# Half-size TensorE tiles in pairs for the half-filled and block-diagonal products of a hybrid decoder's mixing stage

## The chip, the cores and the metric

The kernel runs on one core of a Trainium2 chip. The metric is the time of one launch on the device in microseconds, the median over runs; lower is better.

## The reference

One trunk layer of a decoder with three groups of heads, for 256 prompt tokens and 8 sequences of 8 sample tokens, 320 token columns in all, in fp32:

```
hn = rms_norm(x);  proj = hn @ w_in                     # 2048 -> 6656
y_rw  = rwkv7_mix(...)   # 12 heads x 64: S = S*w_t + (S a_t) b_t' + v_t k_t',  y = S r_t
y_hg  = hgrn2_mix(...)   # 6 heads, 128 x 128 state: S = f_t S + k_t v_t',  o = q_t S
y_lru = rglru_mix(...)   # 512 channels, gated linear recurrence behind a convolution
x = x + concat(y_rw, y_hg, y_lru) @ w_out
hn = rms_norm(x); gate, val = split(hn @ w_up)          # 2 x 5632
x = x + (silu(causal_conv(gate)) * val) @ w_down;  y = rms_norm(x)
```

It returns the outputs of all tokens and the new states of all groups (for HGRN2 `p_hgrn` of the prompt and `s_hgrn` of the samples).

## The kernel before, in words

Channels lie on the 128 partitions, tokens in the free dimension. Every projection (`gemm`) streams its weights in chunks of 8 blocks of 128 x 128 (512 KB) on the SP queue, splits each chunk into a high and a low part on ScalarE (L173) and VectorE (L174), and makes three products of 320 columns for each block: high by high (L198), high by low (L199), and, after the eight blocks of the chunk, low by high (L205). These run on the whole array.

The recurrences are written as products over chunks of 64 tokens. RWKV heads go in pairs, one on each half of the partitions (`half[0]`, `half[1]`); six pairs alternate with six HGRN heads, then two pairs of RG-LRU tiles. Their products are plain fp32. The chains of steps (`rwkv_operands`, `rwkv_chunks`, `rwkv_norm`, `hgrn_steps`, `lru_steps`) are Python generators: `gemm` advances a virtual clock by a fixed cost for each projection product and calls `tick`, which emits the next step of a chain when its due time (the number that it yielded, such as `L_EV = 1.5` or `L_EX = 4.0`) has passed. So steps of the chains are emitted between projection products in a fixed order. The compiler's scheduler then orders each engine's instructions by this order and by when it takes their operands to be ready, and may let an instruction that isn't ready be overtaken by later ones. On the chip each engine goes through its own list in order.

The products that the change and the prediction speak of:

- L445, L447: decay and in-context rate of a pair, `lw` by `lora`. Only 64 of the 128 rows of each stationary operand are not zero (the first half for one, the second for the other).
- L541: products of all pairs of tokens in a chunk, on row halves, into two aux tiles; L551 the same for the samples on the whole array. VectorE masks them into `mt1` and `mt2`. `mt1` goes to DRAM (L569) and back as diagonal 16 x 16 blocks (L570), VectorE inverts these by substitution (L574, L576), and the result goes to DRAM (`du`, L577) and back as `U` (L578). L644 transposes `U` to `T`.
- L584, L594, L603, L610: token-major operands, by products with the identity; L584 on column halves (128x64), L594 on tiles of 64x32, all four into one aux tile, L603 transposes on row halves into two aux tiles.
- L636, L638: the right-hand sides `rq`. For each head and each half of the chunks a transpose on a row half, then a product of `mt2` (zero outside two 64 x 64 blocks) with `vsw`, on the whole array.
- L659, L664, L668: the doubling of the inverse from blocks of 16 to 32 and from 32 to 64. Each is four products with a 128 x 128 operand whose two diagonal 64 x 64 blocks alone are not zero. In the first round L659, L664 and L668 run, in the second L659 and L664.
- L683, L686: `pq` from `U`. L707, L709: outputs without a state, one product on the whole array, one on a column half, alternating. L716: 64x64 tiles, six products.
- L863, L867: HGRN's products of token blocks. L934, L935: transposes of `v` and `kd` to token-major `vt` and `kt`; the 64 sample tokens fill half the rows of the third block, POOL clears the other half (L931). L948 to L953: outputs. L980, L981: `p_hgrn`. L986: the sample states, for four of the eight sequences at a time, `kt` (half filled) by `hex` of 512 columns, which VectorE builds by a mask (L974); L987 adds the result to `hs`, and POOL's queue stores it (L988). L832 loads the next head's `hs` on the same queue.

An aux tile is one PSUM bank of 512 fp32 on 128 partitions. There are four of the kind `aux_r` (RWKV) and two `aux_h` (HGRN, RG-LRU); two more banks are the projections' `acc`.

Of the kernel before, what the change touches and what calls it, by code (L numbers as in the profile page):

```python
# [17 lines left out]
P = 128  # L18
D = 2048
NK = D // P  # L20
TP = 256
# [32 lines left out]
for _name, _w in (  # L54
    ("ident", 128), ("ones", 128), ("bones", 128), ("bswap", 128), 
    ("psw", 128), ("eye2", 64), ("bm", 8), ("bm4", 4),
):
    CST[_name] = (_n, _w)
    _n += _w
# [7 lines left out]
def kernel(ctx: ExitStack, tc: tile.TileContext, i: dict, o: dict):  # L67
# [15 lines left out]
    # ------------------------------------------------------------- constants  # L83
# [12 lines left out]
    # -------------------------------------------------------- weight streaming  # L96
# [29 lines left out]
    def advance(kind):  # L126
        """One more step of the first chain of a kind; False if it waits for something else."""
# [57 lines left out]
    def behind(out, in_):  # L185
        """A load that doesn't go ahead of the weights that are asked for by now."""
        tc.keep_in_program_order(SY.dma_start(out=out, in_=in_))
# [49 lines left out]
    # ------------------------------------------------------------------ input  # L237
# [95 lines left out]
    # ------------------------------------------------------------ RWKV-7 group  # L333
# [54 lines left out]
    # five 128 x 128 matrices in DRAM, with steps that make their diagonal 16 x 16 blocks one pattern  # L388
# [11 lines left out]
    # sample tokens by half of the batches, then by head, block-diagonal in the heads  # L400
# [11 lines left out]
    # the halves of the columns that stay zero  # L412
# [27 lines left out]
    def rwkv_operands(p, lw, box):  # L440
        while state["pairs"] < p - 1:
            yield None
        # decay and in-context rate
        ps_w = aux_r()
        PE.matmul(ps_w[:, :T], lw[:, 0, :], lora, start=True, stop=True)  # L445
        ps_a = aux_r()
        PE.matmul(ps_a[:, :T], lw[:, 1, :], lora, start=True, stop=True)  # L447
# [78 lines left out]
    def rwkv_chunks(p, lw, box):  # L526
# [7 lines left out]
        # products of all pairs of tokens in a chunk  # L534
# [24 lines left out]
        # inverse of the unit triangles: blocks of 16 by substitution, then doubled  # L559
# [20 lines left out]
        # token-major operands  # L580
# [33 lines left out]
        # the sample tokens  # L614
# [16 lines left out]
        rq = rp.tile([P, 4, P], F32, tag="h", name="rq", bufs=BH)  # L631
        for e in range(2):
            ps = aux_r()
            for m in range(2):
                c0 = m * P + e * 64
                PE.transpose(ps[:, c0:c0 + 64], flat(AR[half[e], 0, 2 * m:2 * m + 2, :]), ident[half[e], half[e]])  # L636
                c0 = m * P + (1 - e) * 64
                PE.matmul(ps[:, c0:c0 + 64], mt2[:, 0, 2 * e + m, :], vsw[:, m, (1 - e) * 64:(1 - e) * 64 + 64],  # L638
                          start=True, stop=True)
            S.copy(flat(rq[:, 2 * e:2 * e + 2, :]), ps[:, 0:256])  # L640
# [5 lines left out]
        for h, Z in zip((16, 32), Zs):  # L646
            def part(t, j):
                """Of each 2h columns the first (j = 0) or the second half."""
                return t.rearrange("p b (n j s) -> p b n j s", j=2, s=h)[:, :, :, j, :]
# [5 lines left out]

            yield L_EV
            ps = aux_r()
            for b in range(4):
                PE.matmul(ps[:, b * 64:(b + 1) * 64], mt1[:, 0, b, :], part(Ts[:, b:b + 1, :], 0), start=True, stop=True)  # L659
# [3 lines left out]
            for b in range(4):  # L663
                PE.matmul(ps_u[:, b * 64:(b + 1) * 64], Z[:, b, :], part(Us[:, b:b + 1, :], 1), start=True, stop=True)  # L664
            if h == 16:
                ps_t = aux_r()
                for b in range(4):
                    PE.matmul(ps_t[:, b * 64:(b + 1) * 64], Us[:, b, :], part(Z[:, b:b + 1, :], 0), start=True, stop=True)  # L668
# [32 lines left out]
        # outputs that need no state, and what the state is multiplied with  # L701
        ps_y = aux_r()
        for e in range(2):
            for m in range(2):
                b = 2 * e + m
                c0 = e * 256 + m * P
                PE.matmul(ps_y[:, c0:c0 + P], pq[:, b, :], mt1[:, 1, b, :], start=(b == 0), stop=False,  # L707
                          skip_group_check=True)
                PE.matmul(ps_y[half[1 - e], c0:c0 + P], vsw[:, m, (1 - e) * 64:(1 - e) * 64 + 64],  # L709
                          mt2[:, 1, b, :], start=False, stop=(m == 0), skip_group_check=True)  # L710
# [17 lines left out]
        # states of both heads, block-diagonal with the heads' columns swapped  # L728
# [46 lines left out]
    def rwkv_norm(p, lw, y, bo):  # L775
        yield L_EV
        # group norm, bonus, gate
# [24 lines left out]
    # ------------------------------------------------------------- HGRN2 group  # L802
# [24 lines left out]
    def hgrn_steps(n, box):  # L827
# [28 lines left out]
        def pairs(lhs, rhs, h, w):  # L856
            """Products of the columns' first with their second halves, h wide (all with all if h = 2)."""
# [13 lines left out]
        # blocks of four, from their middles  # L871
# [40 lines left out]
        # b is now summed over each whole sequence  # L912
# [16 lines left out]
        for src, dst in ((v, vt), (kd, kt)):  # L929
            yield L_HG  # L930
            G.memset(dst[64:P, 2, :], 0.0)  # L931
# [3 lines left out]
            PE.transpose(ps[0:64, 2 * P:3 * P], src[:, TP:T], ident)  # L935
            S.copy(dst[:, 0:2, :].rearrange("p a b -> p (a b)"), ps[:, 0:TP])
            S.copy(dst[0:64, 2, :], ps[0:64, 2 * P:3 * P])
# [31 lines left out]
        # states  # L969
        S.activation(dsam, b[:, TP + ST - 1:T:ST], AF.Exp)  # L970
        for q4 in range(2):
            c = slice(4 * q4, 4 * q4 + 4)
            ex = rp.tile([P, 4, P], F32, tag="hb", name="hex", bufs=BHB)
            V.tensor_tensor(ex, bcast(vt[:, 2, :], 4), cc("bm")[:, c].unsqueeze(2).to_broadcast([P, 4, P]), op=ALU.mult)  # L974
            sn = s0[q4]
            V.tensor_tensor(sn, sn, dsam[:, c].unsqueeze(2).to_broadcast([P, 4, P]), op=ALU.mult)
            yield L_EX
            if q4 == 0:
                ps = aux_h()
                PE.matmul(ps[:, 0:P], kt[:, 0, :], vt[:, 0, :], start=True, stop=False)  # L980
                PE.matmul(ps[:, 0:P], kt[:, 1, :], vt[:, 1, :], start=False, stop=True)  # L981
                pst = rp.tile([P, P], F32, tag="hcr", name="pst", bufs=1)
                S.copy(pst, ps[:, 0:P])
                G.dma_start(out=o["p_hgrn"][n], in_=pst)
            ps = aux_h()
            PE.matmul(ps, kt[:, 2, :], ex.rearrange("p b v -> p (b v)"), start=True, stop=True)  # L986
            V.tensor_tensor(sn, ps.rearrange("p (b v) -> p b v", v=P), sn, op=ALU.add)  # L987
            G.dma_start(out=o["s_hgrn"][n, :, c, :], in_=sn)  # L988

    # ------------------------------------------------------------ RG-LRU group  # L990
# [103 lines left out]
    # -------------------------------------------------------- operands of w_out  # L1094
# [37 lines left out]
    # ------------------------------------------------- output projection + norm  # L1132
# [34 lines left out]
    # --------------------------------------------------------------------- FFN  # L1167
# [94 lines left out]
def _constants():  # L1262
# [31 lines left out]
    put("bm", ((r % 64 // 8)[:, None] == np.arange(8)[None, :]).astype(f))  # L1294
# [101 lines left out]
```

## Time and profile before

| | before |
|---|---|
| median of 3 runs | 1670.26 us (1669.49 to 1672.36) |
| profiled execution, its span | 1670.6 us (the page gives no time around it) |
| PE busy | 1636.4 us, 98% |
| weight loads busy | 1588.0 us, 95% |
| VectorE, ScalarE, POOL busy | 989.1 us, 836.3 us, 151.4 us |
| DMA | 238.83 MB, 143 GB/s in the mean |

PE is TensorE's row of matmuls, PEld that of its weight loads, DVE VectorE, ACT ScalarE, POOL GpSimd, SP the queue that streams the weights. An fp32 product leaves two records in the trace, a transpose one. Durations of single records overlap, since products are pipelined; what a group costs is read from the end of one to the end of the next, as the chain of waits does. A shape such as 64*128 is the tile of the array, rows by columns. The mixing stage lies between about 45 and 636 us.

### The profile page before, as it was taken

What the parts mean: (1) busy time and instruction counts of PE and PEld (TensorE: products, weight loads), DVE (VectorE), ACT (ScalarE), POOL (GpSimd) and SP (SyncE); (2) the same over time, 40 slices, a digit from 0 to 9 for tenths busy, and PEclk for the clock granted to TensorE, in tenths of its full rate; (3) what the DMA queues carried; (4) which work ended last, traced back from release to release, by engine and by line L of the source; (5) the groups of instructions that cost most, each with busy time, mean ns of one, the idle gap of its engine ahead of it and who ended that gap; (6) DMA issues with size and microseconds to landing.
All of it is one profiled execution on the core that took longest, in us unless ns stands there. A gap on an engine that the chain in (4) does not pass through costs nothing.

```text
span 1670.6 us, 28501 instructions
## 1 busy us (share of the span) xinstructions
PE 1636.4 (98%) x11220; PEld 1588.0 (95%) x11220; DVE 989.1 (59%) x1958; ACT 836.3 (50%) x1310; POOL 151.4 (9%) x369
## 2 busy tenths in 40 slices
PE   7899999999999999999999999999999999999996
PEld 7898999999899899999999999999999999999996
DVE  7677677777677656555555555333455555554444
ACT  7675767676766774444433343333333444434442
POOL 3001010101010210000000000000000000000000
PEclk9999999999999999999999999999999999999998
DMA  8434343434344445554454554555545555554553
GB/s 269 138 110 122 110 130 109 131 103 120 108 121 117 145 154 161 151 160 148 147 149 151 151 152 146 151 149 152 150 151 151 151 151 150 148 156 147 150 153 106
DMA packets 87101, 238.83 MB, mean 143 GB/s; under 512 B 16568, under 2 KB 30312, under 8 KB 86968
## 3 DMA queue, kind: packets, MB, share of 16 engines
q1 hardware_dynamic: 82072, 221.67, 44.6%
q0 software_dynamic: 4896, 15.36, 2.7%
q8 instruction: 88, 1.44, 0.4%
q14 instruction: 45, 0.37, 0.1%
HBM read 225.62 MB, written 11.37 MB: 142 GB/s over the span
## 4 chain that ended last, share of the span: by engine, by line
PE 93%; DVE 2%; DMA 2%; ACT 2%; issue 1%; SPq 0%; DVEq 0%; ACTq 0%
PE acc L205 27%; PE acc L198 27%; PE acc L199 27%; DMA U<-du 1%; PE aux_h L867 1%; PE aux_h L953 1%; PE aux_r L659 1%; PE aux_h L986 1%; PE aux_r L664 1%; DVE wl L174 1%; PE aux_r L707 1%; PE aux_r L638 1%; PE aux_r L709 1%; DMA xr<-in_xT 0%; DMA raw<-in_w_in 0%
## 5 line engine op out<-in xcount | busy, mean ns | idle before, releaser
L173 ACT CAST wh<-raw 128x1024 fp32r<-128x1024 f32 (+2 forms) x412 | 421.7, 1024 | 526.2 <-PE acc L199 319.5
L198 PE MATMUL acc<-xh,wh 128*128 128x320 f32 x2208 | 671.1, 317 | 1.0 <-DVE ext L342 1.0
L199 PE MATMUL acc<-xl,wh 128*128 128x320 f32 x2208 | 656.3, 310 | 0.0
L174 DVE TENSOR_TENSOR wl<-raw,wh 128x1024 fp32r<-128x1024 f32 (+2 forms) x412 | 489.9, 1190 | 238.2 <-PE acc L205 114.5
L198 PEld LDWEIGHTS acc<-xh,wh 128*128 128x128 f32 x2208 | 416.3, 189 | 6.5 <-issue 2.6
L199 PEld LDWEIGHTS acc<-xl,wh 128*128 128x128 f32 x2208 | 416.4, 189 | 4.2 <-issue 2.4
L205 PE MATMUL acc<-xh,wl 128*128 128x320 f32 x2208 | 385.3, 315 | 0.0
L205 PEld LDWEIGHTS acc<-xh,wl 128*128 128x128 f32 x2208 | 338.1, 189 | 4.1 <-issue 1.1
L198 PE MATMUL acc<-hh,wh 128*128 128x320 f32 x704 | 207.9, 308 | 0.0
L199 PE MATMUL acc<-hl,wh 128*128 128x320 f32 x704 | 207.8, 308 | 0.0
L199 PEld LDWEIGHTS acc<-hl,wh 128*128 128x128 f32 x704 | 132.1, 188 | 0.0
L198 PEld LDWEIGHTS acc<-hh,wh 128*128 128x128 f32 x704 | 131.7, 187 | 0.0
L205 PE MATMUL acc<-hh,wl 128*128 128x320 f32 x704 | 118.8, 308 | 0.0
L1183 POOL COPY ncch<-fe 128x18 f32<-128x18 f32 x44 | 49.1, 1115 | 652.2 <-DVE fe L1182 652.2
L205 PEld LDWEIGHTS acc<-hh,wl 128*128 128x128 f32 x704 | 107.1, 187 | 0.0
L1193 DVE TENSOR_TENSOR fv<-acc,rstd 128x320 f32<-128x320 f32 x44 | 21.6, 492 | 98.3 <-PE acc L205 98.3
L1181 DVE TENSOR_TENSOR fe<-acc,rstd 128x256 f32<-128x256 f32 x44 | 18.7, 425 | 100.3 <-PE acc L205 100.3
L214 ACT CAST hh<-fv 128x320 fp32r<-128x320 f32 x44 | 20.3, 461 | 96.9 <-DVE fv L1195 96.9
L198 PE MATMUL acc<-yhl,wh 128*128 128x320 f32 x224 | 66.1, 309 | 0.5 <-ACT yhl L214 0.5
L199 PE MATMUL acc<-yhl,wh 128*128 128x320 f32 x224 | 66.2, 309 | 0.0
L1188 DVE SCALAR_TENSOR_TENSOR fc<-fe,prm,fc 128x336 f32<-128x336 f32 x88 | 49.7, 565 | 1.6
L1186 ACT ACTIVATE fc<-fe,prm 128x336 f32<-128x336 f32 x44 | 29.5, 669 | 35.5 <-DVE fe L1182 34.7
(414 smaller groups left out, 1723.1 us busy)
## 6 DMA issues: line engine op xcount, KB each, us to landing
raw<-in_w_up SPq DMA_DIRECT2D x176, 512.0 KB
raw<-in_w_in SPq DMA_DIRECT2D x100, 512.0 KB
raw<-in_w_dn SPq DMA_DIRECT2D x64, 512.0 KB
raw<-in_w_out SPq DMA_DIRECT2D x32, 512.0 KB
raw<-in_w_dn SPq DMA_DIRECT2D x32, 384.0 KB
out_s_hgrn<-hs POOLq DMA_DIRECT2D x12, 256.0 KB, 2.6
hs<-in_hs POOLq DMA_DIRECT2D x10, 256.0 KB, 4.5
x<-in_xT POOLq DMA_DIRECT2D x16, 160.0 KB, 3.0
```

The costliest lines, as they stand in the source:

```text
L173: S.copy(wh[:, ks, :], raws[n][:, ks, :])
L174: V.tensor_tensor(wl[:, ks, :], raws[n][:, ks, :], wh[:, ks, :].bitcast(F32), op=ALU.subtract)
L198: PE.matmul(ps[:, :T], wh[:, k, :], xh[k0 + k], start=st, stop=False)
L199: PE.matmul(ps[:, :T], wh[:, k, :], xl[k0 + k], start=False, stop=False)
L205: PE.matmul(ps[:, :T], wl[:, k, :], xh[k0 + k], start=False, stop=en)
L214: S.copy(xh, src)
L638: PE.matmul(ps[:, c0:c0 + 64], mt2[:, 0, 2 * e + m, :], vsw[:, m, (1 - e) * 64:(1 - e) * 64 + 64], start=True, stop=True)
L1181: V.tensor_tensor(e[:, 2:258], ps[:, 0:TP], rstd[:, 0:TP], op=ALU.mult)
L1183: G.tensor_copy(ncch[:, j], e[:, 248:EX].rearrange("p (b s) -> p b s", s=10)[:, :, 8:10])
L1186: S.activation(c[:, 0:N], e[:, 0:N], AF.Identity, scale=pc("fw", 3 * j), bias=pc("fb", j))
L1188: V.scalar_tensor_tensor(c[:, 0:N], e[:, m:m + N], pc("fw", 3 * j + m), c[:, 0:N], op0=ALU.mult, op1=ALU.add)
L1193: V.tensor_tensor(val, ps[:, :T], rstd, op=ALU.mult)
```

## The change

- `rwkv_operands`: the two products take only the filled row half each, one after the other, into two aux tiles.
- rq: first the four transposes, then the products with `mt2`, each as two of 64x64, one for each block that is not zero; then both copies.
- The doubling: a helper `blocks` makes each of the four products as two of 64x64, on the two diagonal tiles, into the two halves of the partitions of one aux tile.
- Outputs without a state: the four whole products first, then the four on column halves.
- HGRN: POOL copies the 64 sample tokens of `v` and `kd` twice side by side (`both`), and the third transpose takes all 128 columns, so that both halves of the rows are filled with the same tokens; ScalarE copies the result in one instruction. `hex` is built once, with a mask that gives the first four sequences to the first half of the rows and the other four to the second. `p_hgrn` is made a step earlier than the sample states, whose two products take one row half each, one after the other, into two aux tiles.

The mask constant `bm` of 8 columns gives way to `bmx` of 4; comments are taken out as well, which is left out here.

```diff
@@ rwkv_operands
-        ps_w = aux_r()
-        PE.matmul(ps_w[:, :T], lw[:, 0, :], lora, start=True, stop=True)
-        ps_a = aux_r()
-        PE.matmul(ps_a[:, :T], lw[:, 1, :], lora, start=True, stop=True)
+        ps_w, ps_a = aux_r(), aux_r()
+        for n, ps in enumerate((ps_w, ps_a)):
+            PE.matmul(ps[:, :T], lw[half[n], n, :], lora[half[n], :], start=True, stop=True)
@@ rwkv_chunks
+        pss = [aux_r(), aux_r()]
+        for m in range(2):
+            for e in range(2):
+                c0 = m * P + e * 64
+                PE.transpose(pss[e][:, c0:c0 + 64], flat(AR[half[e], 0, 2 * m:2 * m + 2, :]), ident[half[e], half[e]])
         for e in range(2):
-            ps = aux_r()
             for m in range(2):
-                c0 = m * P + e * 64
-                PE.transpose(ps[:, c0:c0 + 64], flat(AR[half[e], 0, 2 * m:2 * m + 2, :]), ident[half[e], half[e]])
                 c0 = m * P + (1 - e) * 64
-                PE.matmul(ps[:, c0:c0 + 64], mt2[:, 0, 2 * e + m, :], vsw[:, m, (1 - e) * 64:(1 - e) * 64 + 64],
-                          start=True, stop=True)
-            S.copy(flat(rq[:, 2 * e:2 * e + 2, :]), ps[:, 0:256])
+                for q in range(2):
+                    k, c = half[1 - q], half[q]
+                    PE.matmul(pss[e][c, c0:c0 + 64], mt2[k, 0, 2 * e + m, c], vsw[k, m, (1 - e) * 64:(1 - e) * 64 + 64],
+                              start=True, stop=True)
+        for e in range(2):
+            S.copy(flat(rq[:, 2 * e:2 * e + 2, :]), pss[e][:, 0:256])
...
+            def blocks(ps, lhs, rhs, j):
+
+                for b in range(4):
+                    r = part(rhs[:, b:b + 1, :], j)
+                    for q in half:
+                        PE.matmul(ps[q, b * 64:(b + 1) * 64], lhs[q, b, q], r[q], start=True, stop=True)
+
             yield L_EV
             ps = aux_r()
-            for b in range(4):
-                PE.matmul(ps[:, b * 64:(b + 1) * 64], mt1[:, 0, b, :], part(Ts[:, b:b + 1, :], 0), start=True, stop=True)
+            blocks(ps, mt1[:, 0], Ts, 0)
...
-            for b in range(4):
-                PE.matmul(ps_u[:, b * 64:(b + 1) * 64], Z[:, b, :], part(Us[:, b:b + 1, :], 1), start=True, stop=True)
+            blocks(ps_u, Z, Us, 1)
             if h == 16:
                 ps_t = aux_r()
-                for b in range(4):
-                    PE.matmul(ps_t[:, b * 64:(b + 1) * 64], Us[:, b, :], part(Z[:, b:b + 1, :], 0), start=True, stop=True)
+                blocks(ps_t, Us, Z, 0)
...
-        for e in range(2):
-            for m in range(2):
+        for b in range(4):
+            PE.matmul(ps_y[:, b * P:b * P + P], pq[:, b, :], mt1[:, 1, b, :], start=(b == 0), stop=False,
+                      skip_group_check=True)
+        for m in range(2):
+            for e in range(2):
                 b = 2 * e + m
-                c0 = e * 256 + m * P
-                PE.matmul(ps_y[:, c0:c0 + P], pq[:, b, :], mt1[:, 1, b, :], start=(b == 0), stop=False,
-                          skip_group_check=True)
-                PE.matmul(ps_y[half[1 - e], c0:c0 + P], vsw[:, m, (1 - e) * 64:(1 - e) * 64 + 64],
+                PE.matmul(ps_y[half[1 - e], b * P:b * P + P], vsw[:, m, (1 - e) * 64:(1 - e) * 64 + 64],
                           mt2[:, 1, b, :], start=False, stop=(m == 0), skip_group_check=True)
@@ hgrn_steps
-        for src, dst in ((v, vt), (kd, kt)):
+
+        both = []
+        for src in (v, kd):
+            t = rp.tile([P, 2, TS], F32, tag="both", name="both", bufs=2)
+            G.tensor_copy(t, bcast(src[:, TP:T], 2))
+            both.append(t)
+        for src, t, dst in ((v, both[0], vt), (kd, both[1], kt)):
             yield L_HG
-            G.memset(dst[64:P, 2, :], 0.0)
             ps = aux_h()
             for m in range(2):
                 PE.transpose(ps[:, m * P:(m + 1) * P], src[:, m * P:(m + 1) * P], ident)
-            PE.transpose(ps[0:64, 2 * P:3 * P], src[:, TP:T], ident)
-            S.copy(dst[:, 0:2, :].rearrange("p a b -> p (a b)"), ps[:, 0:TP])
-            S.copy(dst[0:64, 2, :], ps[0:64, 2 * P:3 * P])
+            PE.transpose(ps[:, 2 * P:3 * P], flat(t), ident)
+            S.copy(flat(dst), ps[:, 0:3 * P])
...
+        ex = rp.tile([P, 4, P], F32, tag="hb", name="hex", bufs=BHB)
+        V.tensor_tensor(ex, bcast(vt[:, 2, :], 4), cc("bmx").unsqueeze(2).to_broadcast([P, 4, P]), op=ALU.mult)
         for q4 in range(2):
             c = slice(4 * q4, 4 * q4 + 4)
-            ex = rp.tile([P, 4, P], F32, tag="hb", name="hex", bufs=BHB)
-            V.tensor_tensor(ex, bcast(vt[:, 2, :], 4), cc("bm")[:, c].unsqueeze(2).to_broadcast([P, 4, P]), op=ALU.mult)
-            sn = s0[q4]
-            V.tensor_tensor(sn, sn, dsam[:, c].unsqueeze(2).to_broadcast([P, 4, P]), op=ALU.mult)
-            yield L_EX
-            if q4 == 0:
...
-            ps = aux_h()
-            PE.matmul(ps, kt[:, 2, :], ex.rearrange("p b v -> p (b v)"), start=True, stop=True)
-            V.tensor_tensor(sn, ps.rearrange("p (b v) -> p b v", v=P), sn, op=ALU.add)
-            G.dma_start(out=o["s_hgrn"][n, :, c, :], in_=sn)
+            V.tensor_tensor(s0[q4], s0[q4], dsam[:, c].unsqueeze(2).to_broadcast([P, 4, P]), op=ALU.mult)
+        yield L_EX
+        ps = aux_h()
+        PE.matmul(ps[:, 0:P], kt[:, 0, :], vt[:, 0, :], start=True, stop=False)
+        PE.matmul(ps[:, 0:P], kt[:, 1, :], vt[:, 1, :], start=False, stop=True)
+        pst = rp.tile([P, P], F32, tag="hcr", name="pst", bufs=1)
+        S.copy(pst, ps[:, 0:P])
+        G.dma_start(out=o["p_hgrn"][n], in_=pst)
+        yield L_EX
+        pss = [aux_h(), aux_h()]
+        for q, ps in zip(half, pss):
+            PE.matmul(ps, kt[q, 2, :], flat(ex[q]), start=True, stop=True)
+        for q4, ps in enumerate(pss):
+            V.tensor_tensor(s0[q4], ps.rearrange("p (b v) -> p b v", v=P), s0[q4], op=ALU.add)
+            G.dma_start(out=o["s_hgrn"][n, :, 4 * q4:4 * q4 + 4, :], in_=s0[q4])
```

## Rows read from the trace of the kernel before

**Rows 1.** The page's first line.

```profile
span 1670.6 us, 28501 instructions
```

**Rows 2.** Busy time of one turn: stretch, engines' busy us, granted clock, DMA share, GB/s.

```profile
180.00:264.70 84.70, 84.29 (x602) 77.18 (x602) 62.91 (x173) 57.48 (x111) 10.53 (x25) 1.00 0.41 119
```

**Rows 3.** Waits of PE, whole span: us in total, times, longest.

```profile
PE aux_r L644 <- DMA U<-du: 2.6, 5, 1.1
PE aux_h L986 <- ACT pst L983: 1.3, 1, 1.3
```

**Rows 4.** Chain in order of time, 140 to 170 us: start, us, what.

```profile
148.60 1.09 PE aux_r L541 x16
...
151.50 0.59 PE aux_r L584 x8
...
152.73 0.86 PE aux_h L986 x2
...
154.76 0.25 PE aux_r L594 x8
...
156.38 0.39 PE aux_r L603 x8
156.77 1.36 PE acc L205 x8
...
162.95 1.17 PE acc L205 x8
164.13 0.20 PE aux_r L636
164.33 0.37 PE aux_r L638 x2
```

**Rows 5.** Chain in order of time, 170 to 201 us.

```profile
175.83 4.07 DMA U<-du
...
181.73 1.03 PE aux_r L659 x8
...
183.40 0.93 PE aux_r L664 x8
184.33 0.89 PE aux_r L668 x8
...
189.82 0.84 PE aux_r L664 x8
...
190.88 0.59 PE aux_r L445 x2
191.48 0.54 PE aux_r L447 x2
...
196.88 0.22 PE aux_r L707 x2
197.10 0.36 PE aux_r L709 x2
197.46 0.42 PE aux_r L707 x2
...
199.80 0.38 PE aux_r L716 x12
```

**Rows 6.** Chain in order of time, 213 to 225 us.

```profile
216.32 0.22 PE aux_h L934 x2
216.54 0.11 PE aux_h L935
```

**Rows 7.** Substitution: busy time as in rows 2; an instruction in order of time.

```profile
158.20:169.80 11.60, 11.60 (x70) 10.19 (x69) 10.72 (x36) 6.18 (x12) 1.68 (x4) 1.00 0.62 195
...
159.46 0.67 DVE L987 TENSOR_TENSOR hs<-aux_h,hs 128x512 f32<-128x512 f32 x1
```

**Rows 8.** Waits of POOL, whole span: us in total, times, longest.

```profile
POOL u L566 <- DMA du<-u: 88.3, 5, 29.6
POOL nshift L343 <- DVE ext L342: 70.5, 18, 16.5
```

More of the change, by code (lines that the diff above doesn't have):

```diff
@@ L55 @@
     ("ident", 128), ("ones", 128), ("bones", 128), ("bswap", 128),
-    ("psw", 128), ("eye2", 64), ("bm", 8), ("bm4", 4),
+    ("psw", 128), ("eye2", 64), ("bmx", 4), ("bm4", 4),
 ):
@@ L970, in hgrn_steps @@
         S.activation(dsam, b[:, TP + ST - 1:T:ST], AF.Exp)
+        ex = rp.tile([P, 4, P], F32, tag="hb", name="hex", bufs=BHB)
+        V.tensor_tensor(ex, bcast(vt[:, 2, :], 4), cc("bmx").unsqueeze(2).to_broadcast([P, 4, P]), op=ALU.mult)
         for q4 in range(2):
             c = slice(4 * q4, 4 * q4 + 4)
-            ex = rp.tile([P, 4, P], F32, tag="hb", name="hex", bufs=BHB)
-            V.tensor_tensor(ex, bcast(vt[:, 2, :], 4), cc("bm")[:, c].unsqueeze(2).to_broadcast([P, 4, P]), op=ALU.mult)
-            sn = s0[q4]
-            V.tensor_tensor(sn, sn, dsam[:, c].unsqueeze(2).to_broadcast([P, 4, P]), op=ALU.mult)
-            yield L_EX
-            if q4 == 0:
-                ps = aux_h()
[L980 to L985, printed above, removed]
-            PE.matmul(ps, kt[:, 2, :], ex.rearrange("p b v -> p (b v)"), start=True, stop=True)
-            V.tensor_tensor(sn, ps.rearrange("p (b v) -> p b v", v=P), sn, op=ALU.add)
-            G.dma_start(out=o["s_hgrn"][n, :, c, :], in_=sn)
+            V.tensor_tensor(s0[q4], s0[q4], dsam[:, c].unsqueeze(2).to_broadcast([P, 4, P]), op=ALU.mult)
[13 more added lines that the diff above has]
+            G.dma_start(out=o["s_hgrn"][n, :, 4 * q4:4 * q4 + 4, :], in_=s0[q4])
     cneg = mp.tile([P, NLRU], F32, tag="cneg", name="cneg")
@@ L1293, in _constants @@
     put("bm4", ((r % 32 // 8)[:, None] == np.arange(4)[None, :]).astype(f))
-    put("bm", ((r % 64 // 8)[:, None] == np.arange(8)[None, :]).astype(f))
+    put("bmx", ((r // 8)[:, None] % 8 == 4 * (r // 64)[:, None] + np.arange(4)[None, :]).astype(f))
     m = np.zeros((len(MASKS), P, P), f)
```

## Prediction

> **What bounds the kernel now.** I read the page first, then the busy time by stage, the waits, and last the chain of waits product by product. TensorE (PE) sets the pace of the 1670.6 us span [rows 1]: in one turn of the mixing stage (one RWKV pair beside one HGRN head, 84.7 us) it is busy for 84.29 of 84.70 us at a granted clock of 1.00 (2.4 GHz), with VectorE at 62.91 and ScalarE at 57.48 us [rows 2]. PE waits for almost nothing in the whole run: the one that recurs from turn to turn is at L644, five times for the load of U, 2.6 us in total [rows 3]. So in the mixing stage time is what PE's own instructions take end to end, and a product that gets shorter shortens the run, unless a later product then stands waiting. The projections and the FFN are untouched by the change.
>
> The chain gives the step from the end of one instruction to the end of the next, and so the price of a group with its change of tile size in it [rows 4, 5]. "x8" counts two records for each fp32 product, one for each transpose.
>
> **Prices of half-size tiles.** On the whole array four 64-column products take 0.84 us (L664), 0.21 each, and a 128-column one 0.22 (first L707) [rows 5]. For half-size tiles I assume that two products on different tiles run side by side at the pace of one, 0.22 us per pair for 128 columns and 0.11 for 64. Then L584, two pairs of 128 columns, 0.59 us, leaves 0.15 us for getting into the tile size; L541, four pairs, 1.09 us, leaves 0.21; L594, four products on four tiles at once, 0.25 us, leaves 0.14 [rows 4]; L716, at most two in a row on one tile, 0.38 us, leaves 0.16 [rows 5]. Four shapes agree, so entry is 0.16 us (0.14 to 0.21). Way out: the eight L205 products behind L603 take 1.36 us instead of 1.17, so 0.19 [rows 4]. A run on half-size tiles thus costs 0.35 us beside its products.
>
> **The change part by part**, for one pair or head, then six times.
> 1. *L707 and L709* alternate between whole array and 128x64. Before: 0.22, then 0.36, then three times 0.42 + 0.36, together 2.92 us [rows 5]. After: four whole products, 4 x 0.22, then one run of two pairs, 0.16 + 2 x 0.22, together 1.48; L716 behind it changes tile size either way. Gain 1.44.
> 2. *rq (L636, L638)*. Before: four times 0.20 + 0.37 or 0.36, 2.25 us [rows 4]. After: four transposes on row halves; L603's eight take 0.39 with their entry, so four take 0.16 + 0.12; then eight 64x64 products, four in a row on each of two tiles, 0.16 + 4 x 0.11; way out 0.19. Together 1.07. Gain 1.18.
> 3. *The doubling of the triangles (L659, L664, L668)*, five calls. One call becomes eight 64x64 products, four in a row on each tile: 0.16 + 0.44 + 0.19 = 0.79 us against 0.84. The first call takes 1.03 now, since it follows a half-size L863, so 0.24 gained; L664 and L668 of the first size, 0.93 + 0.89, follow each other and share the way in and out: 0.16 + 0.88 + 0.19 = 1.23, gain 0.59; the last two calls gain 0.05 each [rows 5]. Gain 0.93. Half the arithmetic is gone, but most of it pays for the changes of tile size.
> 4. *HGRN state products (L986)*. Two of 0.86 us [rows 4] become one pair: 0.86 + 0.35 = 1.21. Gain 0.51. The pair needs both aux_h banks, so the p_hgrn product must have been copied out before: PE waited 1.3 us for that copy, once [rows 3], with no projection product between; now a step lies between, so nothing, at most those 1.3 in each head. The second building of hex goes from VectorE; off the path, nothing.
> 5. *Decay and rate (L445, L447)*: 0.59 + 0.54 [rows 5] become 0.54 + 0.35. Gain 0.24.
> 6. *The doubled sample tokens*: L935 takes 0.11 us now [rows 6], the size of a whole transpose here (two L934 in 0.22 [rows 6]), so nothing. ScalarE loses two copies, POOL gets two copies for two memsets. What covers the copies is the step of projections between their issue and the transposes; without that cover PE waits (third rival). The output transfers of hs now leave together on POOL's queue, and the next head's loads of hs behind them are needed most of a head later: nothing.
>
> Sum: 1.44 + 1.18 + 0.93 + 0.51 + 0.24 = 4.30 us, six times 25.8 us. With entry at 0.21 (nine entries) it is 23.1, with 0.14 26.9.
>
> **What is late next.** Between L541, which starts the way to U (masks, DRAM, substitution on VectorE, DRAM again), and L644, which needs U, PE loses parts 2 and 4, 1.69 us. VectorE is busy for 10.72 of 11.60 us in the stretch of the substitution [rows 7], and the load of U is 4.07 us of the chain [rows 5], so U does not come sooner; at five of six pairs PE already waits there [rows 3], so there is no slack. At most 5 x 1.69 = 8.5 us go into that wait; if the second hs update, 0.67 us [rows 7], now always falls inside the substitution, 3.3 more, 11.8 in all. At least nothing is lost: the compiler's scheduler places L644 among projection products by when it thinks U is there, and may put more of them ahead. I take 5, a little below the middle: the waits speak for a loss, the freedom of the order against the whole of it. All other products behind L644 wait for nothing now and have one step of projections between them.
>
> 25.8 - 5 = 20.8 us. The profiled execution's span is 1670.6 us [rows 1]; no time around it is shown, and the median of the runs is 1670.26, 0.02% less. 1670.3 - 20.8 = 1649.5: **forecast 1649.5 us**, own range 1643.4 (26.9 gained, none lost) to 1659 (23.1 gained, 11.8 lost).
>
> **The rivals.**
> *A. Row halves that write one PSUM bank take turns.* The pairs of parts 2 and 3 write both halves of one bank from different row halves; those of L541 and L603 have a bank each. Then each 64x64 pair costs 0.22: the five calls take 1.23, 2.11, 1.23, 1.23 (against 1.03, 1.82, 0.84, 0.84), a loss of 1.27; rq gains 0.74; parts 1, 4, 5 gain 2.19. Together 1.66, six times 10.0, less some 4 of waiting at L644: 1664.3. Against it: L594's four products write one bank from both row halves in 0.25 us, 0.11 beyond the entry [rows 4]; in turns they would need 0.38. Chance 0.10. The Trainium skill, "TensorEngine Tiling (Array Packing)", section Restrictions and Gotchas, states this rule: different row tiles cannot access the same PSUM bank at the same time. By that rule the sum would be rival A's, by the row it is the forecast's; the trace does not agree with the rule here.
>
> *B. The wait for U takes everything it can*: 25.8 - 11.8 = 14.0 are left, 1656.3. For it: no slack now. Against: a new order may fill the wait with projection products. Chance 0.15.
>
> *C. Slower: the copies on POOL.* PE's transposes now wait for a copy on an in-order queue. POOL's head stood waiting for the du store 88.3 us in five cases, up to 29.6 [rows 8]. If the two copies of each head are queued behind such a hold, PE stands at the transposes; above 20.8 / 6 = 3.5 us per head the gain is gone, and at 10 us it is 1649.5 + 60, about 1710. Against it: the holds nearest the transposes are those for ext, 70.5 us over 18, some 4 us each [rows 8], and the scheduler can fill PE meanwhile. Chance 0.03.
>
> *D. The runs are not kept together*: the scheduler mixes projection products into them. Each break costs 0.35 us; eight runs per pair broken once cost 16.8 in all, which with the 5 of waiting leaves 4 of the 25.8; broken a little oftener they take it all: 1668 to 1672. For it: the order is made anew. Against: operands of one run are ready together. Chance 0.06.
>
> **How the numbers follow.** Forecast 0.66, A 0.10, B 0.15, C 0.03, D 0.06. Forecast and B hold 0.81, so the range is 1642 to 1660, which leaves out most of A, C and D. About 0.2% (3.3 us, the spread of the runs shown is 2.9) can be told from no change: faster takes in forecast, B and nearly all of A, 0.90; the same, most of D and the rest of A, 0.06; slower, C and a bit of D, 0.04.
>
> **What would show it.** In the chain: L707 four times 0.22 in a row; each call of the doubling near 0.60 up to its last product, not 0.84 and not 1.04 (rival A); L986 as one pair in about 1.0; the product behind a run 0.15 to 0.2 longer. In the waits: L644 above 2.6 us in total, up to some 14 (B); no wait of the two transposes for POOL (C). In order of time: no projection product inside a run (D). I am wrong if the doubling runs take as long as before, or PE's busy time falls by 26 us and the span does not follow.

## The result, and the profile after

The change made the kernel faster: the median of four runs is 1650.14 us (1647.80 to 1651.69) against 1671.31 us for the kernel before on the same chip (four runs, 1669.49 to 1673.32), a ratio of 0.9878 on record (95% interval 0.9863 to 0.9894; the two medians alone give 0.9873). The forecast was 1649.5 us, the range 1642 to 1660. All medians here leave out one disturbed execution of 3666 us, of one of the kernels below.

The page of the kernel after, its first line and the engines' busy time:

```profile
span 1649.9 us, 29024 instructions
...
PE 1613.8 (98%) x11508; PEld 1567.1 (95%) x11508; DVE 983.7 (60%) x1952; ACT 827.9 (50%) x1293; POOL 154.8 (9%) x369
```

The span is 20.7 us shorter than in [rows 1], and PE's busy time fell by 22.6 us, though there are more instructions. The profiled execution's own time is 1651.69 us, 1.8 us above its span; before, the run of 1672.36 us lies as far above the span of 1670.6, so the difference of spans can be read as a difference of times.

Line numbers shift in the changed kernel: L541 is now L540, L584 L583, L594 L593, L603 L602, L636 and L638 are L635 and L641, L644 is L648, the doubling (L659, L664, L668) is all in L665, L445 and L447 are L446, L707 and L709 are L712 and L717, L716 is L724, L953 is L965, L986 is L998 and L987 is L1000.

Chain of waits in order of time, 154 to 193 us, one turn of mixing; to be laid beside [rows 4, 5]:

```profile
154.27 1.06 PE aux_h L998 x4
...
160.44 0.27 PE aux_r L635 x4
...
160.71 0.61 PE aux_r L641 x16
...
172.04 3.67 DMA U<-du
...
177.54 0.61 PE aux_r L665 x16
178.15 0.64 PE acc L205 x3
178.93 1.08 PE aux_r L665 x32
...
181.89 0.61 PE aux_r L665 x16
...
183.36 0.61 PE aux_r L665 x16
...
184.34 0.74 PE aux_r L446 x4
...
190.97 0.89 PE aux_r L712 x8
191.86 0.59 PE aux_r L717 x8
192.45 0.38 PE aux_r L724 x12
```

Each run stands unbroken, and each is shorter than its counterpart: the outputs 1.48 us for 2.92, rq 0.88 for 2.25, the five calls of the doubling 0.61 + 1.08 + 0.61 + 0.61 = 2.91 for 4.53, the states 1.06 for two of 0.86, the rate 0.74 for 1.13. What the products behind pay for the way out is not in these figures; the busy time of whole turns has it.

Busy time of four turns after (columns as in [rows 2]):

```profile
175.80:257.20 81.40, 80.12 (x650) 73.34 (x651) 62.10 (x171) 55.95 (x108) 10.60 (x25) 1.00 0.42 125
257.20:338.10 80.90, 80.12 (x651) 73.36 (x651) 61.59 (x169) 55.65 (x107) 10.62 (x25) 1.00 0.41 122
338.10:420.90 82.80, 81.65 (x651) 74.74 (x651) 62.38 (x172) 56.28 (x108) 10.60 (x25) 0.98 0.40 123
420.90:503.50 82.60, 81.62 (x650) 74.82 (x651) 61.76 (x170) 55.84 (x107) 9.58 (x20) 0.98 0.40 120
```

At a clock of 1.00 a turn keeps PE busy for 80.12 us; before it was 84.29 [rows 2], so 4.17 less where the prediction has 4.30. Six such turns make 25.0 us. Two things take from it. One is the wait for U, in the waits of PE over the whole span:

```profile
PE aux_r L648 <- DMA U<-du: 5.6, 6, 1.3
```

That is 3.0 us more than in [rows 3]. The other was not foreseen: the last two turns above have a granted clock of 0.98, and PE is busy 1.5 us longer in each. Cut finer, all of that lies in one place in the first of them. Busy time of three stretches of the kernel after, and PE's instructions there in order of time (start, busy us, ..., tile size, shape, count):

```profile
381.00:384.00 3.00, 3.00 (x25) 2.81 (x25) 3.00 (x8) 1.01 (x2) 1.38 (x3) 1.00 0.54 176
384.00:388.00 4.00, 4.00 (x17) 3.72 (x17) 1.54 (x3) 2.33 (x2) 0.85 (x1) 0.57 0.38 132
388.00:391.00 3.00, 3.00 (x28) 2.81 (x29) 1.08 (x3) 2.91 (x4) 0.00 (x0) 1.00 0.52 153
```

```profile
381.49 1.95 PE L965 MATMUL aux_h<-eb,hs 128*128 128x8 f32 x16
...
384.83 2.34 PE L205 MATMUL acc<-xh,wl 128*128 128x320 f32 x8
```

A mean of 0.57 over 4.00 us means that for about 3.4 us PE runs at the lower of its two levels (1.2 instead of 2.4 GHz), although it was busy in all of the 3.00 us before; half of that, 1.7 us, is lost. The fall begins 1.8 to 3.0 us after the first of the eight products of 8 columns that add the old states to a head's sample outputs (L965, before L953), which follow each other within 1.95 us. The trace of before has two such falls (at 397 and 568 us), that of after three (384, 466 and 548 us): one more, 1.7 us. At the start of mixing (46 to 57 us) both traces lose the same, twice 1.7 us, in and behind a wait of some 3 us. Together 25.0 - 3.0 - 1.7 = 20.3 us of the 20.7.

The whole span shows how far this sum is exact: PE is busy 22.6 us less, and its idle time is 36.1 us instead of 34.2. So all waits together grew by 1.9 us and not by 3.0 (one of 3.1 us near the start of mixing is gone, one of 1.0 us there has become 3.2), and the products got shorter by about 24 us in fact: the 22.6, and 1.5 by which the clock costs more over the span of after (its mean is 0.992, before 0.993). The 25.0 carries the two clean turns over to all six.

### The profile page after: what moved, and what is told of

Read it like the earlier page. It is cut to its first block, busy times and chain, and to the rows that moved or that the text cites. A ratio compares the mean times of both kernels' runs of the same rounds, so it can differ in the third digit from the quotient of the medians.

```text
span 1649.9 us, 29024 instructions
## 1 busy us (share of the span) xinstructions
PE 1613.8 (98%) x11508; PEld 1567.1 (95%) x11508; DVE 983.7 (60%) x1952; ACT 827.9 (50%) x1293; POOL 154.8 (9%) x369
## 4 chain that ended last, share of the span: by engine, by line
PE 90%; DVE 3%; DMA 3%; ACT 3%; issue 1%; SPq 0%; DVEq 0%; ACTq 0%
PE acc L205 27%; PE acc L198 27%; PE acc L199 26%; DMA U<-du 1%; PE aux_r L665 1%; PE aux_h L875 1%; DVE wl L174 1%; PE aux_h L965 1%; DMA xr<-in_xT 1%; DMA du<-u 1%; PE aux_r L198 0%; PE aux_h L998 0%; PE aux_r L199 0%; ACT wh L173 0%; DVE x L1234 0%
## 5 line engine op out<-in xcount | busy, mean ns | idle before, releaser
L214 ACT CAST hh<-fv 128x320 fp32r<-128x320 f32 x44 | 20.3, 461 | 96.9 <-DVE fv L1208 96.9
L1199 ACT ACTIVATE fc<-fe,prm 128x336 f32<-128x336 f32 x44 | 29.5, 669 | 35.1 <-DVE fe L1195 35.1
```

The costliest lines, as they stand in the source:

```text
L214: S.copy(xh, src)
L1199: S.activation(c[:, 0:N], e[:, 0:N], AF.Identity, scale=pc("fw", 3 * j), bias=pc("fb", j))
```

## The experiments

Three questions: are the terms of the sum right one by one (theory 1, against the rivals of the prediction), what does the wait for U cost and can it be moved (theory 3, later, is that VectorE sets it), and what do the falls of the clock cost (theory 2). Ratios are to the kernel before on the same chip.

**Outputs alone.** The kernel before with L707's and L709's products no longer alternating:

```
-        for e in range(2):
-            for m in range(2):
...
+        for b in range(4):
+            PE.matmul(ps_y[:, b * P:b * P + P], pq[:, b, :], mt1[:, 1, b, :], ...)
+        for m in range(2):
+            for e in range(2):
...
+                PE.matmul(ps_y[half[1 - e], b * P:b * P + P], vsw[:, m, ...], ...)
```

> The kernel before, with one edit: the four whole L707 products first, then the four half-size L709 products. Theory 1 (every change of tile size has its price on the engine, about 0.2 us each way): L707 0.22 each in a row and the L709 run 0.59 us, 1.44 us less for each pair, 8.6 us in all: 1662, ratio 0.9948. Rival (only the smaller and paired products gain, the order is worth nothing): ratio 1.000.

Measured: 1662.85 us, ratio 0.9959 (0.9944 to 0.9975). Chain, and one turn:

```profile
193.77 0.89 PE aux_r L704 x8
194.66 0.59 PE aux_r L709 x8
```

```profile
430.60:514.00 83.40, 82.83 (x602) 76.59 (x603) 62.47 (x169) 57.10 (x110) 9.52 (x20) 1.00 0.41 118
```

The same eight products take 1.48 us instead of 2.92, and PE's busy time per turn is 82.83 for 84.29, 1.46 less. Nothing but the order has changed, so the price of alternating is shown, together with what the new order also does: it makes neighbours of products on the two column halves, and by the prediction's prices their pairing is 0.44 of its 1.44. A third of the saved busy time (1.46 of 4.17) needs no smaller product.

**Doubling on the whole array.** The kernel after with

```
-                    for q in half:
-                        PE.matmul(ps[q, b * 64:(b + 1) * 64], lhs[q, b, q], r[q], start=True, stop=True)
+                    PE.matmul(ps[:, b * 64:(b + 1) * 64], lhs[:, b, :], r, start=True, stop=True)
```

> The changed kernel, with the doubling products L665 on the whole array again. Theory 1 (half the work, but each run pays 0.35 us for the change of tile size): 0.93 us more for each pair, 5.6 us in all above the changed kernel: 1655.7, ratio 0.991. Rival (the products halve, as their arithmetic does: five calls of 0.84 become 0.42): about 2.1 us for each pair, 12.6 in all: 1663, ratio 0.995.

Measured: 1652.75 us, ratio 0.9894 (0.9879 to 0.9909). One turn:

```profile
340.10:422.10 82.00, 80.95 (x610) 74.90 (x611) 61.80 (x171) 57.10 (x108) 11.64 (x25) 1.00 0.41 122
```

PE is busy for 0.83 us more per turn, 5.0 in six, near the predicted 0.93. The median rose by only 2.6 us. The clock accounts for the rest: the mean granted clock of the four runs is 0.9945, that of the four runs of after 0.9928, which is 2.9 us of 1650, and 5.0 - 2.9 = 2.1. In its trace one fall follows the eight products where after has three.

**Doubling, one tile after the other.** The kernel after with the loops turned round, so that four products go to one tile and then four to the other:

```
-                for b in range(4):
-                    r = part(rhs[:, b:b + 1, :], j)
-                    for q in half:
+                for q in half:
+                    for b in range(4):
+                        r = part(rhs[:, b:b + 1, :], j)
```

> The changed kernel, with the two halves of each doubling call emitted one after the other: four products on the first diagonal tile, then four on the second, instead of in pairs. Theory 1 (products run side by side only when neighbours in the order lie on different tiles): a call takes 0.16 + 0.88 = 1.04 us instead of 0.61, and the double call about 1.9 instead of 1.08; some 2.1 us more for each pair, 12.8 in all: 1663. Rival (TensorE overlaps the tiles of a whole run, in whatever order): 0.61 and 1650.

Measured: 1656.48 us, ratio 0.9911 (0.9895 to 0.9926), between the two. Chain, and one turn:

```profile
178.71 0.89 PE aux_r L665 x16
...
180.38 1.47 PE aux_r L665 x32
```

```profile
177.00:259.40 82.40, 81.34 (x650) 74.53 (x651) 62.17 (x171) 55.90 (x108) 10.64 (x25) 1.00 0.40 123
```

A call takes 0.89 us instead of 0.61, neither the 1.04 of products in turns nor the 0.61 of pairs that find each other in any order. Eight products in turns are 0.16 + 8 x 0.11 = 1.04; the call is 0.15 below that, the double call (0.16 + 16 x 0.11 = 1.92) 0.45, three times as much, and it has three changes from one tile to the other where a single call has one. So products on different tiles ran beside each other only near a change of tile in the order: 0.15 us is the time of one to two products. Per turn that makes 3 x 0.28 + 0.39 = 1.23 us, and the turn shows 1.22. With the doubling on the whole array a turn took only 0.83 us more than after, less than these 1.22: what the half tiles earn in the doubling, the pairing earns.

**The wait for U, first try.** The kernel after with `L_SUB` (how late the transpose of U falls due) at 14.0 instead of 5.0.

> The changed kernel, with the step of L648 due later (L_SUB 14 instead of 5), so that some 14 more projection products stand ahead of L648 in five of six pairs. Theory 1 (the wait for U, 5.6 us, is time that the order loses): the wait falls below 1 us and the run takes 4 to 5 us less: 1645.5, ratio 0.985. Rival (the wait is the way of the pair itself, and what is put ahead only moves it to a later product): the same as the changed kernel, 1650, with new waits behind L648.

Measured: 1651.41 us, ratio 0.9885 (0.9870 to 0.9900), no clear difference from after: the rival. No wait for U is left, but PE has new ones (us in total, times, longest):

```profile
PE aux_h L875 <- DVE at L876: 2.7, 5, 0.6
PE aux_r L446 <- DMA lw<-in_lw: 2.5, 1, 2.5
PE aux_r L743 <- DVE sbd L756: 1.5, 4, 0.4
```

```profile
341.90:423.60 81.70, 80.70 (x652) 73.06 (x651) 61.74 (x171) 55.94 (x108) 9.55 (x25) 1.00 0.40 123
```

This turn takes 81.7 us; the two turns of after at a clock of 1.00 take 81.4 and 80.9. PE waits 1.0 us in it, as much as there (1.3 and 0.8), only behind other steps: a step that is put later pushes the next one into its own wait. And PE is busy 0.6 us longer; where that comes from stays open.

**The falls, by splitting the eight products.** In the kernel after and in the kernel before a step of projections between each two of the eight:

```
         for m in range(SB):
+            if m in (2, 4, 6):
+                yield L_ST
```

After:

> The changed kernel, with a step of projections between each two of the eight 8-column products (L965 in the changed kernel, L967 here; L953 before). In all traces so far the granted clock falls to 0.50 for about 3.4 us only in some turns, and within the mixing stage nearly always right after these eight products in a row; one fall costs 1.7 us. Theory 2 (these eight products in a row make the clock fall, in the changed kernel oftener than in the one before): no fall at this place any more, mean clock from 0.992 to 0.995 or more, 3 to 5 us less than the changed kernel: 1646, ratio 0.985. Rival (the falls come from the mixing stage as a whole, now thinner in products): falls stay at other places, 1650.

Measured: 1659.36 us, ratio 0.9938 (0.9926 to 0.9951). Before:

> The kernel before, with the same split of the eight 8-column products. Theory 2: falls of the clock at this place go here too, about one or two of them in a run: 2 to 3 us less, 1668, ratio 0.9985. Rival: 1.000. The difference between the changed kernel's gain by this edit and this one's is what the change gives back in the clock.

Measured: 1672.75 us, ratio 1.0017 (1.0008 to 1.0025). In both traces no fall is left behind the eight products, and both kernels lose. That the falls went is not luck of one trace: the mean granted clock of the eleven runs of the split kernel before is 0.9962, that of the fifteen runs of before beside them 0.9942, a difference worth 3.3 us of 1671. In the split kernel before, a turn without a fall:

```profile
348.50:434.10 85.60, 84.70 (x603) 77.42 (x604) 62.29 (x172) 55.96 (x109) 9.43 (x25) 1.00 0.40 117
```

```profile
PE aux_r L644 <- DMA U<-du: 4.5, 5, 1.1
```

PE is busy 0.4 us longer per turn than in [rows 2], 2.5 us in six, and waits 1.9 us longer for U: 4.4 us against the 3.4 of the two falls. In the split kernel after the three more steps took cover away: in the turn below PE works 27.0 us from the start of L540 to L648 where it works 29.5 in after, and U, though there 0.9 us sooner after L540, is waited for longer. Its waits, and PE's order of time (the bracket is the idle time ahead):

```profile
PE aux_r L648 <- DMA U<-du: 12.1, 5, 2.9
```

```profile
423.24 0.63 PE L648 MATMUL aux_r<-cst,U 128*128 128x128 f32 x4 [2.72 <-DMA U<-du]
```

```profile
423.20:507.00 83.80, 81.79 (x651) 74.39 (x652) 61.49 (x170) 55.68 (x107) 10.17 (x20) 0.98 0.38 116
```

The clock of the turn that begins there is 0.98 with no fall behind the eight products (L967 here): it falls right behind the wait, at 423 us, and so at another at 256 us. These two waits, of 2.7 and 2.9 us, cost a fall on top; the other three, of 2.0 to 2.5 us, did not.

**Splitting, and U earlier.** The split kernel after without the `yield L_FILL` behind the copies of `vsw` and of `uv`, so that L583, L593 and L602 go out as one step.

> The split of the eight products, and in RWKV the steps of L583, L593 and L602 emitted as one, so that runs of half-size tiles follow each other. Theory 1: at least one way out less for each pair, 0.2 us, 1.2 in all, below split_outputs: 1645. Rival: the four aux_r banks run out and PE waits for a copy of vsw or vs: 1646 to 1650, with that wait in the trace.

Measured: 1675.34 us, ratio 1.0035 (1.0022 to 1.0049), a miss:

```profile
PE aux_r L646 <- DMA U<-du: 20.3, 6, 4.0
```

The steps taken away were cover: in the second pair PE works only 25.8 us between L540 and the transpose (27.0 in the split kernel), and U is there no sooner. Five of the six waits, of 3.5 to 4.0 us, have a fall in or right behind them; the first, of 2.2 us, has none. PE waits for no copy of `vsw` or `vs`, so the rival did not come true either.

**States on the whole array.** The kernel after with the HGRN transposes and states of before. Two kernels with the same edit; the trace is the second's.

> The changed kernel, with the HGRN part as before (third transpose half filled, hex built twice, two L986 products on the whole array in two steps). By the chain the pair of row halves takes 1.06 us and a way out, against 2 x 0.86: theory 1 gives 0.47 more per head, 2.8 us in all: 1653, ratio 0.9895. Rival (the copies on POOL and the second update of hs inside the substitution cost as much as the pair gains): 1650, with a smaller wait for U.

> The same kernel as whole_states, whose profiled run was disturbed. Theory 1: 0.47 us more per head than the changed kernel, 2.8 in all, 1653 at the same clock. Rival: 1650, the wait for U at L648 smaller by about 0.6 us in each of five pairs, since one of the two hs updates of 0.67 us no longer stands ahead of the substitution.

Measured: 1648.22 us (three runs, 1648.04 to 1651.69), ratio 0.9877 (0.9862 to 0.9892), and 1649.18, ratio 0.9878 (0.9860 to 0.9897). From the trace:

```profile
256.80:338.30 81.50, 80.60 (x651) 73.79 (x652) 62.50 (x172) 55.94 (x109) 9.54 (x25) 1.00 0.42 123
```

```profile
PE aux_r L648 <- DMA U<-du: 5.3, 5, 1.2
```

PE's busy time is 0.48 above the 80.12 of after, 0.44 in the next turn: the term (0.51) is there. The medians don't show it, since the clock hides it: no fall follows the eight products in this trace where after has three. The spans fit: 2.8 us for six turns less 5.1 for three falls is -2.3, and the spans are 1647.6 and 1649.9 us. The wait for U stays: the pair of row halves takes 0.5 us of PE's work out of the way to L648, but U also comes 0.5 us sooner with it (30.5 us after the start of L540 instead of 31.0, in the mean of five turns).

**The eight products in two groups.** The kernel after with four of them behind each group of transposes (L943 on), ahead of the attention product:

```
+        ps_o = aux_h()
+        for n4, (src, t, dst) in enumerate(((v, both[0], vt), (kd, both[1], kt))):
...
+            for m in range(4 * n4, 4 * n4 + 4):
+                PE.matmul(ps_o[:, ...], s0[m // 4][:, m % 4, :], eb[:, ...], start=True, stop=False, ...)
```

> The changed kernel, with the eight 8-column products (L965) in two groups of four, behind the two groups of transposes, two steps earlier than now; the head's chain gets no longer by it. Theory 2 (the eight in a row make the clock fall, 1.7 us each time, three times in the trace of the changed kernel): no fall at this place, the wait for U as in the changed kernel (5 to 6 us), 3 to 5 us less: 1646.5, ratio 0.9855. Rival (the falls only move to another place, since the split also brought new ones): 1650.

Measured: 1645.66 us, ratio 0.9854 (0.9839 to 0.9869). In this kernel and in the last one the HGRN heads' sample outputs don't hold their whole sum, whose products are begun at several places of one bank here; number and size of PE's products are as in after.

```profile
254.40:335.40 81.00, 79.97 (x651) 73.32 (x651) 61.93 (x171) 55.92 (x107) 10.02 (x25) 1.00 0.42 124
```

```profile
PE aux_r L648 <- DMA U<-du: 5.1, 5, 1.1
```

The four turns from 173 to 497 us take 81.0 us each at a clock of 1.00, none has a fall, and the wait for U is nearly as before this edit. The median is 4.5 us below that of after. By the mean granted clock of four runs each (0.9948 and 0.9928) some 3.3 us of that are the clock; about 1 us more is that PE is busy 0.15 us less per turn. So theory 2 held where the split cost no time by itself. But the falls don't follow each such row: states on the whole array kept the row and had none. A form that keeps the whole sum was not run, so no better kernel is claimed.

**The substitution on POOL.** The kernel after with its 30 operations per pair (L573, L575) on POOL, since VectorE is nearly full in that stretch:

> The changed kernel, with the 30 small products and sums of the substitution (L573, L575) on POOL instead of VectorE. Theory 3 (the wait for U is set by VectorE, busy 11.2 of 12.5 us between the start of the substitution and its end): U comes earlier, the wait falls from 5.6 us to below 2, and since L648 stands earlier in the order too, the run takes 3 to 5 us less: 1646.5, ratio 0.9855. Rival (POOL takes longer for each of the 30 than the order assumes; no row shows such an operation there): the wait grows, some 0.2 us more each would be 6 us a pair and 1670 or above.

Measured: 1711.22 us, ratio 1.0247 (1.0232 to 1.0263). One line's instructions, after and then here (count: min/median/max ns), and the wait here:

```profile
L573 DVE TENSOR_TENSOR t<-n,u x90: 157/197/219, 76.9 to 495.1; 40x15 f32<-40x15 f32 x12, 40x28 f32<-40x28 f32 x12, 40x39 f32<-40x39 f32 x12, 40x48 f32<-40x48 f32 x12
```

```profile
L573 POOL TENSOR_TENSOR t<-n,u x90: 207/296/1384, 75.7 to 549.8; 40x15 f32<-40x15 f32 x12, 40x28 f32<-40x28 f32 x12, 40x39 f32<-40x39 f32 x12, 40x48 f32<-40x48 f32 x12
```

```profile
PE aux_r L648 <- DMA U<-du: 54.1, 6, 9.6
```

The wait for U is ten times as long, 9.6 us instead of 1.1 in the second pair, for two reasons. POOL takes half as long again for each of these small operations, so U is there 33.7 us after the start of L540 instead of 30.5. And the order put L648 37 PE instructions earlier, so PE works only 24.1 us ahead of it instead of 29.5. Over the span PE is idle for 83.4 us instead of 36.1 and, at a mean clock of 0.975, busy 12.6 us longer. Whether VectorE sets the wait (theory 3) stays open by this run, since POOL was the slower engine. With the eight products in two groups as well:

> Both edits of early_outputs and substitution_on_pool. Theory 2 and theory 3 together: 6 to 9 us less than the changed kernel, 1643, ratio 0.983. If only one holds: about 1646.5; if POOL is too slow: as substitution_on_pool, less what the clock gives.

Measured: 1709.14 us, ratio 1.0230 (1.0215 to 1.0246), the same picture.

## Why the prediction was right, point by point

**What bounds it.** PE was the bound and stayed it: of the 24 to 25 us that its products got shorter 20.7 came out in the span, and the rest is found on PE itself, in waits and in its clock.

**Prices.** The entry of 0.16 us and pairs at the pace of one product held: a call of the doubling takes 0.61 where 0.60 was worked out, the joined one 1.08 for 1.04, the states 1.06 for 1.02 (without the way out), the rate 0.74 for 0.70, the outputs 1.48 for 1.48. rq gains 1.37 less the way out of 0.19, so 1.18 as predicted. The doubled sample tokens cost nothing that the turns show.

**The terms.** By busy time the outputs are 1.46 (1.44 predicted), the doubling 0.83 (0.93), the states 0.45 (0.51). rq and the rate had no run of their own; what is left for them, 4.17 - 1.46 - 0.83 - 0.46 = 1.42, is what the prediction has (1.18 + 0.24). The sum, 4.17 a turn for 4.30, is 25.0 us for 25.8, inside the bounds of 23.1 to 26.9; so are the 24 of the whole span.

**The wait for U** is the step that was mis-sized: 5 us taken, 3.0 measured (bounds 0 to 11.8). That the time goes into this wait was right: it now comes in all six pairs. What PE loses ahead of L644 was right too. Busy time from the start of L541 (in after L540) to the wait, before and after, and the product that waits:

```profile
148.53:179.73 31.20, 31.20 (x220) 28.04 (x219) 25.44 (x68) 18.66 (x38) 3.92 (x10) 1.00 0.55 160
180.04 0.63 PE L644 MATMUL aux_r<-cst,U 128*128 128x128 f32 x4 [0.31 <-DMA U<-du]
```

```profile
145.31:174.79 29.48, 29.48 (x228) 26.70 (x227) 24.56 (x67) 18.29 (x37) 4.70 (x9) 1.00 0.57 166
175.84 0.63 PE L648 MATMUL aux_r<-cst,U 128*128 128x128 f32 x4 [1.05 <-DMA U<-du]
```

PE works 1.72 us less there, where the prediction has 1.69, and it is the same in each of the last five turns. What failed is the sentence that U does not come sooner: it is there 30.53 us after the start of L540 instead of 31.51 after that of L541, and 1.2 us sooner in the mean of the five turns. So of 5 x 1.7 us only 2.7 became waiting, and 0.4 more came in the first pair. Nor did the second hs update fall inside the substitution. In before it stood inside, behind the first product [rows 7]; in after both updates stand in a row ahead of it. VectorE's first product of before, its last sum, and the same of after:

```profile
159.37 0.17 DVE L574 TENSOR_TENSOR t<-n,u 40x15 f32<-40x15 f32 x1
171.40 0.17 DVE L576 TENSOR_TENSOR u<-u,t 40x15 f32<-40x15 f32 x1
```

```profile
155.36 1.29 DVE L1000 TENSOR_TENSOR hs<-aux_h,hs 128x512 f32<-128x512 f32 x2
156.57 0.16 DVE L573 TENSOR_TENSOR t<-n,u 40x15 f32<-40x15 f32 x1
167.58 0.17 DVE L575 TENSOR_TENSOR u<-u,t 40x15 f32<-40x15 f32 x1
```

The substitution begins 0.4 us later after L540 in this turn and takes 11.2 us instead of 12.2; it ends 0.6 us sooner, and so it does in all five. The other 0.6 us of the 1.2 lie behind it, in the store and the load of U (the load is 3.67 us of the chain here, 4.07 in [rows 5]); what made these shorter was not isolated.

**The clock** was not in the prediction at all: one more fall, 1.7 us, made up for most of the 2 us by which the wait was taken too high. So it is partly luck that the forecast of 1649.5 came so near to 1650.14: it is better than its parts. Whether the changed kernel's clock falls oftener by nature is open: the granted clock of its four runs was 0.992 to 0.994 (mean 0.9928), that of the 33 runs of before beside the experiments 0.992 to 0.997 (mean 0.9943), and traces with the eight products together have from three falls behind them (after) to none (states on the whole array).

**The rivals.** A, row halves that write one bank take turns: a call would take 1.04 us and takes 0.61, so the pairs of 64x64 products that write two halves of one bank do run side by side. The Trainium skill, "TensorEngine Tiling (Array Packing)", section Restrictions and Gotchas, has the rule that different row tiles cannot access the same PSUM bank at the same time. The 0.61 us don't agree with it for tiles that write different halves of the partitions. The prediction's own row of evidence (L594) carried over. What did matter is the order (0.89 us when a tile's four products stand together), and the sum would have lost 6 x 1.22 = 7.3 us by it. B, the whole 11.8 us into the wait: 5.6 in all, 3.0 added. C, copies on POOL: PE waited for none. D, runs broken up: none is.

## What to carry to other kernels

Where TensorE is the bound, price a product by the chain with its change of tile size in it: a run on half-size tiles costs some 0.35 us beside its products here, so group products of one size first (that, with the pairs it makes, was a third of this gain), and let neighbours in a run sit on different tiles. When the bound gets shorter, look for what was just in time before; here it took 3 of 25 us, and neither attempt to move or shorten that wait (the transpose later, the substitution on POOL) gained anything. And compare the granted clock of the same stretch in both traces before a difference of 2 us is put down to an edit.

## What the runs showed of the hardware that was not expected

- Products on two tiles overlap by neighbourhood: eight 64x64 fp32 products take 0.61 us alternating between two tiles, 0.89 us as four and four, where the one change between tiles saves about 0.15 us against the 1.04 worked out for products in turns.
- The granted clock fell to 1.2 GHz for about 3.4 us with PE busy throughout, behind eight fp32 products of 8 columns in a row (1.95 us). Kernels that split the row had no fall there, kernels that kept it had none to three in six heads. Waits of 2.7 to 4.0 us for U had a fall in or behind them too, those of 2.0 to 2.5 us had none (one of 2.5 us for `lw`, with L_SUB at 14.0, had one). The Trainium skill, "TensorE: Matmul & The Clock Gate", section "Part 1: The HAM clock gate", lets the clock follow how busy the engine has been. The longer waits agree with that; the eight products don't by their records, since PE shows as busy for all of the 3.00 us ahead of the fall.
- A small elementwise operation (40 partitions, 15 to 64 elements) took 0.296 us on POOL against 0.197 on VectorE in the median, and up to 1.38.
